# Weight sums of the Strassen products: adding DMAs from GpSimd's queue instead of VectorE

## The chip, the cores and the metric

The kernel runs on one core of a Trainium2 chip. The metric is the device time of one execution in microseconds (us), the median of several runs. The engines are called PE (TensorE, matmuls; PEld is its weight load), DVE (VectorE), ACT (ScalarE), POOL (GpSimd) and SP (SyncE, which here only issues DMAs). PEq, ACTq, SPq and POOLq are the instruction queues of these engines.

## The reference

A trunk of two layers over 512 tokens of width 1024, in float32. Each layer is a half-step feed-forward block, a mixer, a second half-step feed-forward block and a gated input embedding; a final norm follows.

```python
def swiglu(x, w_gu, w_down):
    g, u = jnp.split(x @ w_gu, 2, axis=-1)
    return (jax.nn.silu(g) * u) @ w_down
...
    for i in range(DEPTH):
        h = h + 0.5 * swiglu(rmsnorm(h, ffn1_norm[i]), ffn1_w_gu[i], ffn1_w_down[i])
        u = rmsnorm(h, mix_norm[i])
        b_g, c_g, v_c, q_c, kv_c, k_r, g_conv, g_mla = jnp.split(u @ w_in[i], split_pts, axis=-1)
        y_conv = short_conv_branch(b_g, c_g, v_c, conv_w[i], w_conv_out[i])
        y_mla = mla_branch(q_c, kv_c, k_r, ...)
        merged = jax.nn.sigmoid(g_conv) * y_conv + jax.nn.sigmoid(g_mla) * y_mla
        h = h + merged @ w_o[i]
        h = h + 0.5 * swiglu(rmsnorm(h, ffn2_norm[i]), ffn2_w_gu[i], ffn2_w_down[i])
        gate = jax.nn.sigmoid(rmsnorm(h, ple_norm[i]) @ w_ple_gate[i])
        h = h + gate * (p[i] @ w_ple_proj[i])
    return rmsnorm(h, final_norm)
```

What matters here are the products `x @ w_gu` of the four feed-forward blocks (w_gu is 1024 x 5632) and the two gate products of the mixer (columns g_conv and g_mla of w_in).

## The kernel before, in words

Activations are kept transposed: a tile holds 128 features (partitions) by 512 tokens. Every float32 operand is split into a high part (a cast to float32r, on ACT) and a low part (the difference, on DVE), and each product is made of three matmuls: high by high, high by low, low by high.

Weights lie in HBM as pieces of 128 x 1024 float32 (512 KB), in the order of their use. `Stream.raw` (L45) loads a piece from SP's queue into one of ten buffers, named `st` (`N_RAW`, L29); `Stream.split` (L61) casts it to `wh` on ACT (L67) and takes the difference `wl` on DVE (L68). There are four buffers each of `wh` and `wl` (`N_WH`), so the splits run at most some three pieces ahead of TensorE. A load waits until the split of the piece that held its buffer has read it.

Most of the gate and up products are made by the Strassen scheme in Winograd's form, seven products in place of eight. A unit of it, called a quad here, is four pieces of weights: the quarters a11, a21, a22, a12 of a block of 512 columns by 1024 rows (a first index for the group of columns, a second for the half of the rows). There are 47 quads: 9 in the first feed-forward block (named a0 in the profile), 10 in each of the other three (b0, a1, b1), 4 in each of the two mixers (m0, m1). The names of the products in PSUM have the block, the number of the quad and the letter of the bank: a07c is bank c of quad 7 in block a0.

The inputs of the seven products come from `Halved.row` (L353): sums and differences of the left and right 256 tokens of the upper and lower features, named x, y, t and u. `Quad.part(j)` (L119) gives the weights of product j and takes the weight sums on DVE: L127 makes `s` = a21 + a22 in a fifth buffer for product 5, L132 takes a11 from it for product 6, L135 takes `s` from a12 for product 3, L138 takes a21 from a11 for product 7. `Sevens.product` (L394) makes the 24 matmuls of 128 x 256 (L400), and `Sevens.step` (L403) gathers the results: products 1, 5 and 6 are copied out of PSUM on ACT (L419), products 2, 3 and 7 are added on DVE (L424), and four finished quarters of the output go to `finish` (L462) or `gate` (L611). There DVE multiplies by the row factor r of the norm (L466, L613), and ACT takes SiLU or sigmoid.

In a feed-forward block the products of neighbouring quads are woven into one another, with parts of the down projection between them (`down`, L479, 12 matmuls of 128 x 512 each):

```python
for i, (n_, j_) in enumerate(((n + 1, 1), (n, 7), (n + 1, 5), (n, 4), (n + 1, 2), (n + 1, 6), (n + 1, 3))):
    step(n_, j_)
    if i in (1, 2, 3, 5) and between:
        between.pop(0)()
```

So in the steady state, product 6 of a quad is followed by one `down`, then by product 3. The first quad of a block runs its products 1, 2, 5, 6, 3 in a row, and in b0, a1 and b1 the second quad has no `down` between its products, as `between` is still empty (n of 1, L515); there the inputs of the quads and the norm are also made. The mixer does the same with `conv_out` in place of `down`.

The order of each engine's instructions is fixed when the program is built, by a scheduler that follows the order of the text as a priority and lets an instruction pass that it expects to be ready sooner. At run time each engine goes through its own list in order.

Of the kernel before, what the change touches and what calls it, by code (L numbers as in the profile page):

```python
# [13 lines left out]
ALU = mybir.AluOpType  # L14
AX = mybir.AxisListType

P = 128
# [15 lines left out]
class Stream:  # L33


    def __init__(self, nc, src, sp, wp):
        self.nc, self.src, self.sp, self.wp = nc, src, sp, wp
        self.halves = []
        self.tiles = None
        self.ahead = []  # L40
# [70 lines left out]
class Quad:  # L111


    def __init__(self, W, quarters):
        self.W = W
        for q in ("a11", "a21", "a22", "a12"):
            setattr(self, q, W.raw(quarters[q]))

    def part(self, j):  # L119

        W = self.W
        tt = W.nc.vector.tensor_tensor
        if j == 1:
            return W.split(self.a11)
        if j == 5:
            self.s = W.buffer("s")
            tt(self.s, self.a21, self.a22, ALU.add)  # L127
            return W.split(self.s)
        if j == 2:
            return W.split(self.a12)  # L130
        if j == 6:
            tt(self.s, self.s, self.a11, ALU.subtract)  # L132
            return W.split(self.s)
        if j == 3:
            tt(self.a12, self.a12, self.s, ALU.subtract)  # L135
            return W.split(self.a12)
        if j == 7:
            tt(self.a11, self.a11, self.a21, ALU.subtract)  # L138
            return W.split(self.a11)
        return W.split(self.a22)  # L140


def pack(halves, n_halves, arrays):
# [15 lines left out]
def trunk_kernel(ctx, tc, dims, x, p, positions, gains, rope_c, weights, out):  # L159

    nc = tc.nc
    S, D, DEPTH, PD, DFF, CONV, QL, KL = dims
# [11 lines left out]
    W = Stream(nc, weights, sp, wp)  # L174

    def G(name, dt=F32):
        return gp.tile([P, S], dt, tag="g", name=name)
# [60 lines left out]
    def gain(nm, l, k):  # L238
        c = col_at[nm, l] + k
        return cols[:, c:c + 1]  # L240
# [4 lines left out]
    class Squares:  # L245
# [5 lines left out]
        def add(self, t):  # L251
            w = t.shape[1]
            if self.acc is None:
                self.acc = G(self.name + "acc")[:, :w]
                nc.scalar.activation(self.acc, t, AF.Square)
                return
            sq = G(self.name + "sq")[:, :w]
            nc.scalar.activation(sq, t, AF.Square)
            nc.vector.tensor_tensor(self.acc, self.acc, sq, ALU.add)
# [86 lines left out]
    class Halved:  # L346
# [6 lines left out]
        def row(self, j, xs):  # L353
            H = S // 2
            left, right = slice(0, H), slice(H, S)
            name, k = self.name, j + KD // 2

            def halves_of(hi_lo, *ps_):
                for at, p_ in zip((left, right), ps_):
                    if p_:  # L360
                        self.ys[p_].append(tuple(t[:, at] for t in hi_lo))

            xj, xk, t13, t24 = (G(f"{name}{w}{j}") for w in "xytu")
            nc.scalar.mul(xj, h[j], gain(self.nm, self.l, j))
            nc.scalar.mul(xk, h[k], gain(self.nm, self.l, k))
            halves_of(xs[j], 1, None)
            halves_of(xs[k], 2, 3)
            nc.vector.tensor_tensor(t13[:, left], xj[:, right], xj[:, left], ALU.subtract)
            nc.vector.tensor_tensor(t13[:, right], xk[:, right], xj[:, right], ALU.subtract)
            nc.vector.tensor_tensor(t24[:, left], t13[:, right], xj[:, left], ALU.add)  # L370
            nc.vector.tensor_tensor(t24[:, right], xk[:, left], t24[:, left], ALU.subtract)
            halves_of(split(t13, f"{name}t{j}"), 5, 7)
            halves_of(split(t24, f"{name}u{j}"), 6, 4)

    class Sevens:
# [5 lines left out]
        H = S // 2  # L381
# [21 lines left out]
        def step(self, n, j):  # L403
# [18 lines left out]
            else:  # L422
                i, f, c = {2: (1, 0, 0), 3: (6, 0, 1), 7: (5, 1, 1)}[j]
                nc.vector.tensor_tensor(d[i], ps, d[i], ALU.add)  # L424
                self.done(n, f, c, d[i], d[i])

    def ffn(l, nm, name, first=False, beside=None, early=False):
        H = S // 2
        nf = DFF // P
        W.close()  # L430
        acts = {}
        ys = Halved(nm, l, name)
        n_early = KD // 2 - 2 if early else 0

        def early_rows(k, xs):
            if KD // 2 < k + 1 <= KD // 2 + n_early:
                ys.row(k - KD // 2, xs)

        xs, acc = normed(nm, l, name, early_rows)


        n_whole = 4 if first else 2
        cs = [[W.col(nm + "_w_gu", l, c + f * P, D) for c in (0, DFF)] for f in range(n_whole)]
        names = [[f"{name}p{w}{f}" for w in "gu"] for f in range(n_whole)]
        n = 2 if first else 1
        pss = projs(sum(cs[:n], []), xs, sum(names[:n], []))
        r = rms(acc, D, name)
        for f in range(n, n_whole):
            pss += projs(cs[f], xs, names[f])
        for j in range(n_early, KD // 2):  # L450
            ys.row(j, xs)

        def activate(f):
            g, u = G(f"{name}gn{f}"), G(f"{name}un{f}")
            nc.vector.tensor_tensor(g, pss[2 * f], r, ALU.mult)
            nc.scalar.activation(g, g, AF.Silu)
            nc.vector.tensor_tensor(u, pss[2 * f + 1], r, ALU.mult)
            nc.vector.tensor_tensor(u, u, g, ALU.mult)
            acts[f] = split(u, f"{name}a{f}")


        def finish(n, f, c, src, t):  # L462

            i = 2 * n + f
            at = slice(c * H, (c + 1) * H)
            nc.vector.tensor_tensor(t, src, r[:, at].unsqueeze(1).to_broadcast([P, 2, H]), ALU.mult)  # L466
            nc.scalar.activation(t[:, 0, :], t[:, 0, :], AF.Silu)
            whole = i in acts
            if not whole:
                acts[i] = G(f"{name}an{i}")  # L470
            nc.vector.tensor_tensor(acts[i][:, at], t[:, 1, :], t[:, 0, :], ALU.mult)
            if whole:
                acts[i] = split(acts[i], f"{name}a{i}")

        sevens = Sevens(nm + "_w_gu", l, name, ys.ys, lambda n: [[c + (2 * n + a_) * P for c in (0, DFF)] for a_ in range(2)],
                        finish)
        step = sevens.step

        def down(m, f0, f1, ps=None, last=True, first_=True):  # L479
            ps = PS(f"{name}pd{f0}_{m}") if ps is None else ps  # L480
            for f in range(f0, f1):
                mm3(ps, W.get((nm + "_w_down", l, f * P, m * P)), acts[f], first_ and f == f0, last and f == f1 - 1)
            if last:
                nc.vector.scalar_tensor_tensor(h[m], ps, 0.5, h[m], ALU.mult, ALU.add)  # L484
            return ps

        np_ = nf // 2
        n0 = n_whole // 2
        for f in range(n_whole - 2):
            activate(f)  # L490
        step(n0, 1)
        activate(n_whole - 2)
        step(n0, 2)
        step(n0, 5)
        activate(n_whole - 1)
        step(n0, 6)
        step(n0, 3)
        for n in range(n0, np_):
            f0 = (n - 2) // 2 * 4
            if n == np_ - 1:  # L500

                pds = []
                for i, j in enumerate((7, 4, None)):
                    pds.append(down(i, f0, f0 + 4, last=False))
                    if j:
                        step(n, j)
                if beside:
                    beside()
                for m in range(KD):
                    if m < 3:  # L510
                        down(m, f0 + 4, nf, pds[m], first_=False)
                    else:
                        down(m, f0, nf)
                break
            between = [(lambda m=m, f0=f0: down(m, f0, f0 + 4)) for m in range(4 * (n % 2), 4 * (n % 2) + 4)] if n > 1 else []  # L515
# [4 lines that stand above are left out]
# [12 lines left out]
    def mixer(l):  # L532
# [32 lines left out]
        for k, (vh, vl) in enumerate(xs):  # L565
            if k % 4 == 0:
                wa, wb = W.halves_of(*kr_cols[k:k + 4])
            t = slice(k % 4 * P, (k % 4 + 1) * P)
            nc.tensor.matmul(pkr, wa[:, t], vh, start=k == 0, stop=False)
            nc.tensor.matmul(pkr, wb[:, t], vl, start=False, stop=k == KD - 1)  # L570
        r = rms(acc, D, name)
# [38 lines left out]

        def gate(n, f, c, src, t):  # L611
            at = slice(c * (S // 2), (c + 1) * (S // 2))
            nc.vector.tensor_tensor(t, src, r[:, at].unsqueeze(1).to_broadcast([P, 2, S // 2]), ALU.mult)  # L613
            for w in range(2):
                i = 4 * n + 2 * f + w
                if gates[i] is None:
                    gates[i] = G(f"{name}g{i}")
                nc.scalar.activation(gates[i][:, at], t[:, w, :], AF.Sigmoid)
# [149 lines left out]
        for m in range(KD):  # L768
            mla_part(m, N_HEADS - 2 if m < 3 else 0, N_HEADS)
            t = m_b[m]  # L770
# [172 lines left out]
```

## Time and profile before

| | us |
|---|---|
| median of 3 runs | 2305.26 (2304.94 to 2305.39) |
| the profiled execution's own time | 2305.14 |
| its span, first to last instruction | 2303.4 |
| TensorE busy | 2281.0 |
| VectorE busy | 1881.2 |
| ScalarE busy | 1129.3 |
| GpSimd busy | 36.8 |

The profile shows one execution. A row of the groups has the line, the engine, the operation, output and inputs, shape and count, then the busy time in us and the mean ns of one, then the idle time of the engine before it and what ended that. A row of the waits has the waiting engine, tile and line, what it waited for, the sum in us, the times, and the longest. A row of the timeline has the start and the duration in us. A row of the DMA issues has the size and the median us from issue to landing. The granted TensorE clock was 0.996 of full speed on average.

### The profile page before, as it was taken

Reading aid. Unit: us, or ns where it says so; the run is one execution under the profiler, and the core shown is the slowest. Engines: PE = TensorE matmul, PEld = TensorE weight load, DVE = VectorE, ACT = ScalarE, POOL = GpSimd, SP = SyncE. Lnnn points to the kernel's source line nnn. Section 1 sums busy time; section 2 is a strip of 40 time slices with the busy share of each in tenths; the row PEclk is TensorE's granted clock in tenths of the full one; section 3 lists DMA queues with packets and bytes.
Section 4 is the critical chain, followed back from the end, with each engine's and each line's share of the span. In section 5 each row is a group of like instructions: output and inputs, shape, how many; then the busy total and the mean of one; then the engine's idle time right before and its main releaser. Section 6 shows DMA issues by size and latency. Waiting matters only on the chain.

```text
span 2303.4 us, 34969 instructions
## 1 busy us (share of the span) xinstructions
PE 2281.0 (99%) x14272; PEld 2068.1 (90%) x14272; DVE 1881.2 (82%) x2613; ACT 1129.3 (49%) x1683; POOL 36.8 (2%) x42
## 2 busy tenths in 40 slices
PE   9999999999999999999999999999999999999997
PEld 7999988899888999998899999889988889999987
DVE  8978779978966988877898887689789579888776
ACT  7444444455644644444564444445466355444455
POOL 0000000000100000000000000000002000000000
PEclk9999999999999999999999999999999999999998
DMA  5333343233122233334223333322331213333341
GB/s 193 110 110 100 102 124 101 66 109 119 46 74 83 81 112 92 110 109 130 73 83 110 96 106 111 119 92 64 120 101 47 83 55 120 101 101 110 120 137 38
DMA packets 64529, 228.03 MB, mean 99 GB/s; under 512 B 7408, under 2 KB 7408, under 8 KB 64368
## 3 DMA queue, kind: packets, MB, share of 16 engines
q1 hardware_dynamic: 63936, 225.47, 31.5%
q8 instruction: 112, 1.84, 0.3%
q14 instruction: 49, 0.40, 0.1%
q10 hardware_dynamic: 432, 0.32, 0.0%
HBM read 223.66 MB, written 2.10 MB: 98 GB/s over the span
## 4 chain that ended last, share of the span: by engine, by line
PE 93%; DVE 5%; ACT 1%; issue 1%; DMA 0%; ACTq 0%; SPq 0%
PE a0pd L198 2%; PE b0pd L198 2%; PE b1pd L198 2%; PE a1pd L198 2%; PE a1pd L199 2%; PE b0pd L199 2%; PE a0pd L199 2%; PE b1pd L199 2%; PE a1pd L200 2%; PE b1pd L200 2%; PE a0pd L200 2%; PE b0pd L200 2%; DVE wl L68 1%; PE e1gp L198 1%; PE e1gp L199 1%; PE e1gp L200 1%
## 5 line engine op out<-in xcount | busy, mean ns | idle before, releaser
L67 ACT CAST wh<-st 128x1024 fp32r<-128x1024 f32 (+1 forms) x471 | 490.8, 1043 | 588.0 <-issue 66.4
L68 DVE TENSOR_TENSOR wl<-st,wh 128x1024 fp32r<-128x1024 f32 (+1 forms) x471 | 570.1, 1211 | 159.7 <-ACT wh L67 159.1
L67 ACT CAST wh<-s 128x1024 fp32r<-128x1024 f32 x94 | 98.8, 1051 | 120.2 <-PE b0pd L199 8.5
L68 DVE TENSOR_TENSOR wl<-s,wh 128x1024 fp32r<-128x1024 f32 x94 | 114.4, 1217 | 13.4 <-ACT wh L67 13.3
L135 DVE TENSOR_TENSOR st<-st,s 128x1024 f32<-128x1024 f32 x47 | 57.4, 1222 | 1.1
L132 DVE TENSOR_TENSOR s<-s,st 128x1024 f32<-128x1024 f32 x47 | 57.3, 1218 | 0.2
L138 DVE TENSOR_TENSOR st<-st,st 128x1024 f32<-128x1024 f32 x47 | 57.2, 1217 | 0.1
L127 DVE TENSOR_TENSOR s<-st,st 128x1024 f32<-128x1024 f32 x47 | 57.1, 1216 | 0.1
L484 DVE SCALAR_TENSOR_TENSOR h<-b0pd,h 128x512 f32<-128x512 f32 x40 | 27.5, 688 | 9.1 <-PE b0pd L200 9.1
L484 DVE SCALAR_TENSOR_TENSOR h<-b1pd,h 128x512 f32<-128x512 f32 x40 | 27.5, 688 | 9.1 <-PE b1pd L200 9.1
L484 DVE SCALAR_TENSOR_TENSOR h<-a1pd,h 128x512 f32<-128x512 f32 x40 | 27.5, 687 | 7.5 <-PE a1pd L200 7.5
L484 DVE SCALAR_TENSOR_TENSOR h<-a0pd,h 128x512 f32<-128x512 f32 x40 | 27.5, 687 | 6.4 <-PE a0pd L200 6.4
L103 POOL MEMSET wh<- 128x256 f32 x4 | 1.1, 314 | 1195.1 <-DVE wl L68 1195.1
L771 DVE TENSOR_TENSOR m0g<-m0mop,m0g 128x512 f32<-128x512 f32 x8 | 5.5, 691 | 6.5 <-PE m0mop L200 6.5
L771 DVE TENSOR_TENSOR m1g<-m1mop,m1g 128x512 f32<-128x512 f32 x8 | 5.5, 691 | 6.2 <-PE m1mop L200 6.2
L272 ACT ACT_TABLE_LOAD x8 | 10.3, 1283 | 0.1
L776 DVE TENSOR_TENSOR h<-m1wop,h 128x512 f32<-128x512 f32 x8 | 5.5, 691 | 4.1 <-PE m1wop L200 4.1
L776 DVE TENSOR_TENSOR h<-m0wop,h 128x512 f32<-128x512 f32 x8 | 5.5, 690 | 4.1 <-PE m0wop L200 4.1
L824 ACT ACTIVATE e_0g<-e_0g 128x512 f32<-128x512 f32 (+1 forms) x13 | 6.8, 529 | 2.8 <-DVE e_0g L823 2.7
L861 PE MATMUL ft<-ident,fh 128*128 128x128 f32 x32 | 5.9, 322 | 1.8 <-DVE fh L853 1.8
L198 PE MATMUL a0pg<-a0x0h,wh 128*128 128x512 f32 x4 | 2.2, 551 | 5.5 <-ACT a0x0h L193 5.5
L622 DVE TENSOR_TENSOR m0g<-m0cop,m0g 128x512 f32<-128x512 f32 x8 | 5.5, 690 | 2.5 <-PE m0cop L200 2.5
(11091 smaller groups left out, 8854.5 us busy)
## 6 DMA issues: line engine op xcount, KB each, us to landing
st<-in_weights SPq DMA_DIRECT2D x416, 512.0 KB, 3.6
st<-in_weights SPq DMA_DIRECT2D x8, 256.0 KB, 5.4
h<-in_x SPq DMA_DIRECT2D x8, 256.0 KB, 5.4
out<-fo SPq DMA_DIRECT2D x8, 256.0 KB, 2.3
e0pi<-in_p SPq DMA_DIRECT2D x2, 256.0 KB, 4.0
e1pi<-in_p SPq DMA_DIRECT2D x2, 256.0 KB, 3.8
pos_i<-in_positions ACTq DMA_DIRECT2D x1, 256.0 KB, 4.3
cols<-in_gains ACTq DMA_DIRECT2D x1, 53.0 KB, 2.9
```

What stands on the lines that cost most here:

```text
L67: self.nc.scalar.copy(hi[:, w], src[:, w])
L68: self.nc.vector.tensor_tensor(lo[:, w], src[:, w], hi[:, w].bitcast(F32), ALU.subtract)
L127: tt(self.s, self.a21, self.a22, ALU.add)
L132: tt(self.s, self.s, self.a11, ALU.subtract)
L135: tt(self.a12, self.a12, self.s, ALU.subtract)
L138: tt(self.a11, self.a11, self.a21, ALU.subtract)
L198: nc.tensor.matmul(ps, wh, vh, start=first, stop=False)
L199: nc.tensor.matmul(ps, wh, vl, start=False, stop=False)
L200: nc.tensor.matmul(ps, wl, vh, start=False, stop=last)
L484: nc.vector.scalar_tensor_tensor(h[m], ps, 0.5, h[m], ALU.mult, ALU.add)
L771: nc.vector.tensor_tensor(t, mla_ps[m], t, ALU.mult)
L776: nc.vector.tensor_tensor(h[m], ps, h[m], ALU.add)
```

## The change

The weight sums leave VectorE. `Quad.__init__` loads the four quarters as before, and then `s` is no buffer of its own but a21, into which a DMA from GpSimd's queue adds a22, read from HBM a second time (`accum_op`). After the split for product 1, a DMA adds a21 from HBM into a11, for product 7. After the split for product 5, one adds a11 into `s`, for product 6; after that for product 6, one adds a12 into `s`, for product 3. Each adds 512 KB. A DMA adds and does not subtract, so the signs move: the weights of products 5, 6, 3 and 7 are now sums alone, the input differences t and u are taken with the signs that belong to it, and the second half of each quad's outputs (f = 1) comes out with its sign reversed. `scaled` turns it back where the outputs are multiplied by the row factor. The instructions there and in `row` stay as many as before. The numbers of buffers and the order of the steps in the text are as before.

```diff
     def __init__(self, W, quarters):
-        self.W = W
+        self.W, self.at = W, {}
         for q in ("a11", "a21", "a22", "a12"):
+            self.at[q] = len(W.halves)
             setattr(self, q, W.raw(quarters[q]))
+        self.s = self.a21
+        self.add(self.s, "a22")
+
+    def add(self, t, q):
+        self.W.nc.gpsimd.dma_start(out=t, in_=self.W.src[self.at[q]], accum_op=ALU.add)
 
     def part(self, j):
 
         W = self.W
-        tt = W.nc.vector.tensor_tensor
         if j == 1:
-            return W.split(self.a11)
-        if j == 5:
-            self.s = W.buffer("s")
-            tt(self.s, self.a21, self.a22, ALU.add)
-            return W.split(self.s)
-        if j == 2:
-            return W.split(self.a12)
-        if j == 6:
-            tt(self.s, self.s, self.a11, ALU.subtract)
-            return W.split(self.s)
-        if j == 3:
-            tt(self.a12, self.a12, self.s, ALU.subtract)
-            return W.split(self.a12)
-        if j == 7:
-            tt(self.a11, self.a11, self.a21, ALU.subtract)
-            return W.split(self.a11)
-        return W.split(self.a22)
+            res = W.split(self.a11)
+            self.add(self.a11, "a21")
+            return res
+        if j in (5, 6):
+            res = W.split(self.s)
+            self.add(self.s, "a11" if j == 5 else "a12")
+            return res
+        return W.split({2: self.a12, 3: self.s, 7: self.a11, 4: self.a22}[j])
...
-            nc.vector.tensor_tensor(t13[:, left], xj[:, right], xj[:, left], ALU.subtract)
+            nc.vector.tensor_tensor(t13[:, left], xj[:, left], xj[:, right], ALU.subtract)
             nc.vector.tensor_tensor(t13[:, right], xk[:, right], xj[:, right], ALU.subtract)
-            nc.vector.tensor_tensor(t24[:, left], t13[:, right], xj[:, left], ALU.add)
-            nc.vector.tensor_tensor(t24[:, right], xk[:, left], t24[:, left], ALU.subtract)
+            nc.vector.scalar_tensor_tensor(t24[:, left], t13[:, right], -1.0, xj[:, left], ALU.mult, ALU.subtract)
+            nc.vector.scalar_tensor_tensor(t24[:, right], t24[:, left], -1.0, xk[:, left], ALU.mult, ALU.subtract)
...
+    def scaled(t, src, f, r):
+
+        r = r.unsqueeze(1).to_broadcast([P, 2, S // 2])
+        if f == 0:
+            nc.vector.tensor_tensor(t, src, r, ALU.mult)
+        else:
+            nc.vector.scalar_tensor_tensor(t, src, -1.0, r, ALU.mult, ALU.mult)
...
-            nc.vector.tensor_tensor(t, src, r[:, at].unsqueeze(1).to_broadcast([P, 2, H]), ALU.mult)
+            scaled(t, src, f, r[:, at])
...
-            nc.vector.tensor_tensor(t, src, r[:, at].unsqueeze(1).to_broadcast([P, 2, S // 2]), ALU.mult)
+            scaled(t, src, f, r[:, at])
```

## The prediction

> **What bounds the kernel now.** I read the head of the page first, then the waits of TensorE, then the groups of the lines that the change touches, then the timeline around one Strassen quad in the steady state and one at the start of a feed-forward block.
>
> ```profile
> span 2303.4 us, 34969 instructions
> PE 2281.0 (99%) x14272; PEld 2068.1 (90%) x14272; DVE 1881.2 (82%) x2613; ACT 1129.3 (49%) x1683; POOL 36.8 (2%) x42
> PE a0pg L198 <- ACT a0x0h L193: 5.5, 1, 5.5
> PE fss L850 <- DVE f0acc L259: 2.4, 1, 2.4
> PE fss L850 <- DVE f256acc L259: 1.9, 1, 1.9
> PE ft L861 <- DVE fh L853: 1.8, 2, 1.6
> ...
> PE b01c L400 <- ACT b01c L419: 0.6, 1, 0.6
> PE b11c L400 <- ACT b11c L419: 0.6, 1, 0.6
> PE a11b L400 <- DVE wl L68: 0.5, 1, 0.5
> ```
>
> TensorE is busy in 2281.0 of 2303.4 us. Its large waits are one at the start (5.5) and a few in the final norm (2.4, 1.9, 1.8). In the Strassen products (L400) it waits 0.6 + 0.6 + 0.5 = 1.7 us in all, each time at the start of a feed-forward block. VectorE is the second engine with 82%, but it is not what the end waits for. So the change takes work off an engine that hardly holds TensorE up, and it can give back little more than those 1.7 us, with small stalls beside them perhaps 3 us. The question is what the new DMAs cost.
>
> **What is removed.** The four weight sums of a quad, on VectorE:
>
> ```profile
> L135 DVE TENSOR_TENSOR st<-st,s 128x1024 f32<-128x1024 f32 x47 | 57.4, 1222 | 1.1
> L132 DVE TENSOR_TENSOR s<-s,st 128x1024 f32<-128x1024 f32 x47 | 57.3, 1218 | 0.2
> L138 DVE TENSOR_TENSOR st<-st,st 128x1024 f32<-128x1024 f32 x47 | 57.2, 1217 | 0.1
> L127 DVE TENSOR_TENSOR s<-st,st 128x1024 f32<-128x1024 f32 x47 | 57.1, 1216 | 0.1
> ```
>
> 57.4 + 57.3 + 57.2 + 57.1 = 229.0 us of VectorE work goes, 188 instructions in 47 quads. In the steady state none of it lies on the path that sets the end. At the start of a block it nearly does, as VectorE is full there:
>
> ```profile
> 762.00:800.00 38.00, 37.35 (x302) 36.52 (x301) 37.53 (x51) 24.14 (x35) 0.00 (x0) 1.00 0.29 87
> 830.00:1040.00 210.00, 210.00 (x1460) 196.75 (x1459) 167.95 (x203) 91.56 (x122) 0.00 (x0) 1.00 0.35 106
> ```
>
> The columns are the stretch, its length, then busy time of TensorE, its weight load, VectorE, ScalarE and GpSimd. In 762 to 800 us VectorE is busy 37.53 of 38.00 us and TensorE loses 0.65; in 830 to 1040 us VectorE has 42 us spare and TensorE loses nothing. The instructions that change their form (the reversed signs in `row` and `scaled`) keep their count and their elements, so I cost them at nothing.
>
> **What is added.** 188 DMAs of 512 KB on GpSimd's queue, each adding a quarter of the weights from HBM into a buffer in SBUF. The trace has no adding DMA, and none from GpSimd. The nearest rows are the plain loads of the same quarters from SyncE's queue:
>
> ```profile
> st<-in_weights SPq DMA_DIRECT2D x416, 512.0 KB, 3.6
> DMA to landing us min/median/max: 2.8/3.6/10.2
> q1 hardware_dynamic: 63936, 225.47, 31.5%
> ```
>
> A plain load lands 3.6 us after its issue, between 2.8 and 10.2 (the latter in the burst at the start). An adding DMA must also read its destination. The third row gives the packets of that queue, their MB and their share of 16 engines' time: a packet takes 31.5% x 16 x 2303.4 / 63936 = 0.18 us of one DMA engine, and a 512 KB load has 128 rows, 8 packets on each of 16 engines: 1.45 us. If the second read costs as much as the first, my estimate for an add, L, is 3.6 + 1.45 = 5.1 us; the ends are 2.8 (it costs no more than the quickest load) and 10.2 + 1.45 = 11.7. I take 5.1, since nearly all loads lie near their median. The share of the DMA engines rises by 188 x 2.9 us / 2303 = 24 points, from a third to a half or more: room enough.
>
> The Trainium skill ("DMA: Bandwidth & Descriptors", section on the anatomy of a DMA of the GpSimd path) fits such a DMA as 2.0 us plus its bytes at 436 GB/s. That would be 3.2 us for 512 KB, below the 3.6 us of the row, and an estimate of 4.4 us with the bytes counted twice; no trace here shows it, and by it each late product below would be 0.7 us less late.
>
> Three of the four adds have time: the one of a22 into a21 runs when both quarters are due long before product 5; that of a21 into a11 starts after product 1 is split and is used most of a period later by product 7; that of a11 lies between products 5 and 6, with other products between. If that cover were gone, each would cost what the next one may cost. The tight one is the add of a12 into `s`, between the split for product 6, which must have read `s`, and the split for product 3, which reads the sum. Before, L135 needed only the old `s`, so it ran ahead of the split. Now there is a chain. In the steady state:
>
> ```profile
> 205.37 1.05 ACT L67 CAST wh<-s 128x1024 fp32r<-128x1024 f32 x1 [1.06 <-PE a0pd L199]
> 206.86 1.22 DVE L68 TENSOR_TENSOR wl<-s,wh 128x1024 fp32r<-128x1024 f32 x1
> 208.39 1.05 ACT L67 CAST wh<-st 128x1024 fp32r<-128x1024 f32 x1 [1.97 <-PE a06b L400]
> 209.48 1.23 DVE L68 TENSOR_TENSOR wl<-st,wh 128x1024 fp32r<-128x1024 f32 x1 [0.31 <-ACT wh L67]
> ...
> 219.52 0.28 PE L400 MATMUL a07c<-a0x4h,wh 128*128 128x256 f32 x1
> ```
>
> The first two rows are the split for product 6 of quad 7, the next two that for product 3, the last the first matmul of product 3; its third matmul, 0.24 us later, needs the low part. `s` has been read at 208.08; a split takes 209.48 + 1.23 - 208.39 = 2.3 us. So L may be 219.52 + 0.24 - 208.08 - 2.3 = 9.4 us, some 9.1 with the hand-over, before TensorE waits. At 5.1 us the add is hidden with 4 us to spare. What queues behind the waiting cast on ScalarE (the SiLU of product 4, the copy of product 6) is needed later than product 3. On VectorE the low part of the split waits with it, and that engine has the freed 1.22 us slots. On GpSimd's queue a waiting add holds the next add, and GpSimd has only 36.8 us of other work. SyncE's loads stay on their own queue, and a quad now holds four buffers instead of five, so they come no later.
>
> At the start of a block the second quad has no `down` between products 6 and 3, and splits run less far ahead:
>
> ```profile
> 783.91 1.21 DVE L68 TENSOR_TENSOR wl<-st,wh 128x1024 fp32r<-128x1024 f32 x1
> 787.71 1.22 DVE L132 TENSOR_TENSOR s<-s,st 128x1024 f32<-128x1024 f32 x1
> 791.51 1.21 DVE L68 TENSOR_TENSOR wl<-s,wh 128x1024 fp32r<-128x1024 f32 x1
> ...
> 793.40 0.28 PE L400 MATMUL b02b<-b0u0h,wh 128*128 128x256 f32 x1
> 796.28 0.28 PE L400 MATMUL b02c<-b0x4h,wh 128*128 128x256 f32 x1
> 799.16 0.28 PE L400 MATMUL b03b<-b0x0h,wh 128*128 128x256 f32 x1
> ...
> 1925.59 1.21 DVE L68 TENSOR_TENSOR wl<-s,wh 128x1024 fp32r<-128x1024 f32 x1
> 1930.35 0.28 PE L400 MATMUL b12c<-b1x4h,wh 128*128 128x256 f32 x1
> ...
> 1184.16 1.22 DVE L68 TENSOR_TENSOR wl<-s,wh 128x1024 fp32r<-128x1024 f32 x1
> 1197.98 0.28 PE L400 MATMUL a12c<-a1x4h,wh 128*128 128x256 f32 x1
> 1165.21 1.21 DVE L68 TENSOR_TENSOR wl<-s,wh 128x1024 fp32r<-128x1024 f32 x1
> 1177.00 0.28 PE L400 MATMUL a12b<-a1x0h,wh 128*128 128x256 f32 x1
> 1177.24 0.28 PE L400 MATMUL a11c<-a1x4h,wh 128*128 128x256 f32 x1
> ```
>
> In b0, `s` is free for the add of a12 at 791.51 + 1.21 = 792.7; with L = 5.1 and the split's 2.3 the low part is there at 800.1, and product 3 wants it at 796.28 + 0.24: 3.6 us late if the order of the work stays. In b1 the same from 1926.8: 3.6. In a1 two adds follow the split for product 5, done at 1185.4: 1185.4 + 2 x (5.1 + 2.3) = 1200.2, against 1198.2: 2.0. For the first quad of a1, 1166.4 + 14.8 = 1181.2 against 1177.5: 3.7. Sum with the order kept: 3.6 + 3.6 + 2.0 + 3.7 = 12.9 us. But the order of the work is no fixed text: the last two rows show a matmul of the next quad's product 1 (a12b) ahead of product 3 (a11c), so work that is ready is put into such gaps when the program is laid out. In b0 the next quad's product 1 stands at 799.16, right behind, 2.88 us long (799.16 - 796.28). Put ahead four times it covers 2.9 + 2.9 + 2.0 + 2.9 = 10.7 of the 12.9 us. About 2 us stay.
>
> **The sum**, against the profiled execution's own 2305.14 us (span 2303.4 and 1.7 around it; the median of the runs, 2305.26, is the same within 0.01%): nothing in the steady state, about 2 us more and 1.7 us less at the starts. I allow 1.5 us for uneven landings: 2307.
>
> **The rivals.** A measurement of this kernel can tell about 0.2% from no change, 4.6 us.
>
> First, slower, at the starts: the adds take longer than the layout of the program allowed for, so no product is moved ahead and every late split is paid. With 5.1 us that is 12.9 us, 2318; with L = 8 each add makes a product 2.9 us later, twice where two adds follow one another, some 6 times: 12.9 + 17 = 30, 2335. Against it stands the filling in the rows above; for it, that VectorE's fullness there makes splits late already. The Trainium skill's page "SBUF — State Buffer" (section on who interferes with whom) speaks against the change here: a VectorE instruction in a two-port mode keeps GpSimd from writing descriptors. No run here shows it yet. By the rows a wait for one VectorE instruction in progress is up to 1.22 us, which makes L 6.3: hidden in the steady state, and 5 to 7 us more in this case (1.22 us at the four late products, twice at two of them).
>
> Second, slower, in the steady state: if L passes 9.1 us, product 3 waits in every quad with a `down` before it, 36 of the 47 (8 or 9 in each of four blocks, one or two in each mixer). It decides from 9.1 on: at the upper end, 11.7, it is 2.6 x 36 = 94 us, 2399. If the add ran at a quarter of a load's rate or in many small pieces, L would be 15 or more and the price over 200 us. For it speaks that nothing in the trace shows an adding DMA; against it that even the slowest load took 10.2.
>
> Third, faster: VectorE is no longer full at the starts, and the waits there (1.7 us, and the 0.65 us of each such stretch) go; with adds near the lower end, 2.8 us, nothing is late. That is 2305.1 - 3 = 2302, still within what can be told; over 4.6 us would need gains that TensorE's waits do not hold.
>
> **How the numbers follow.** Hidden, within 0.2%: 0.47. Late at the starts: 0.25, slower. Late in the steady state: 0.20, slower, and 0.03 of it far above. Faster by over 0.2%: 0.05; the remaining 0.03, for a cost that I have not named (the start and end of GpSimd's queue), goes to slower. So faster 0.05, same 0.47, slower 0.48: the likeliest single case is no change, 2307, with its own range of 2301 to 2309.7; slower has as much chance spread over two cases. The range that holds 8 in 10 runs from 2301 to 2400: below it lie few of the faster cases, above it the longest adds, 0.12 or so.
>
> **What would show it.** VectorE's busy time falls by 229 us to about 1652, TensorE's stays at 2281. Adds land in about 5 us. TensorE shows no wait before product 3 in the steady state, and waits of a few us at most at 760 to 800, 1160 to 1204 and 1896 to 1934 us. Wrong would be landings over 9 us with a wait before product 3 in each period; a product order at the starts that is unchanged; or ScalarE's casts waiting for DMAs long enough that later splits are late too.

## The result and the profile after

The change makes the kernel slower: 2345.62 us (median of 4 runs, 2343.57 to 2347.05) against 2305.32 us, a ratio of 1.0175 with a 95% interval of 1.0162 to 1.0188. The profiled execution's span is 2345.1 us against 2303.4, 41.7 us more. Two executions on record took far longer than all the others (3793.81 us of the run with useless matmuls below, 7995.75 us of the kernel before); the ratios leave them out.

From the page of the changed kernel: the span, the busy time, the new DMA queue (packets, MB, share of 16 engines) and the issues; the last row, from the view of line L123, has the landing of the adds.

```profile
span 2345.1 us, 35365 instructions
PE 2296.3 (98%) x14272; PEld 2082.1 (89%) x14272; DVE 1683.1 (72%) x2425; ACT 1124.0 (48%) x1683; POOL 200.6 (9%) x230
q0 software_dynamic: 27072, 98.58, 24.4%
st<-in_weights SPq DMA_DIRECT2D x416, 512.0 KB, 4.0
st<-in_weights POOLq DMA_DIRECT2D x188, 512.0 KB, 5.7
DMA to landing us min/median/max: 5.2/5.7/10.8
```

VectorE lost 198 us of work, TensorE got 15 us more busy with the same 14272 matmuls, and an add lands 5.7 us after its issue. TensorE's waits (engine, tile, line, what it waited for: us, times, longest) say where the time went:

```profile
PE a11c L396 <- ACT wh L67: 4.3, 1, 4.3
PE b01c L396 <- ACT wh L67: 4.2, 1, 4.2
PE b11c L396 <- ACT wh L67: 3.9, 1, 3.9
PE m1g0c L396 <- ACT m1g0c L415: 3.8, 1, 3.8
PE m0g0c L396 <- ACT m0g0c L415: 3.8, 1, 3.8
PE a02c L396 <- ACT a02c L415: 3.6, 1, 3.6
...
PE a12c L396 <- ACT wh L67: 2.3, 1, 2.3
```

These are single waits, one in each of the six blocks, all ahead of product 3 of the block's first quad, and one more in the second quad of a1. Short waits for the low part of the same split follow (0.5 to 0.7 us in four of these places), and b02c and b12c wait 0.2 us for theirs; the view lists none in the other quads. Busy time by stretch (length, TensorE, its weight load, VectorE, ScalarE, GpSimd, then the granted clock, the DMA share and GB/s):

```profile
466.00:482.00 16.00, 12.21 (x89) 12.00 (x88) 9.21 (x10) 10.16 (x14) 1.73 (x2) 0.89 0.70 156
785.00:800.00 15.00, 10.09 (x61) 9.62 (x60) 10.11 (x13) 7.71 (x10) 1.73 (x2) 0.77 0.63 138
1221.00:1232.00 11.00, 8.15 (x43) 7.79 (x43) 8.58 (x12) 6.79 (x10) 1.76 (x2) 0.69 0.59 119
200.00:330.00 130.00, 130.00 (x891) 121.17 (x890) 86.37 (x110) 55.85 (x75) 10.46 (x12) 1.00 0.63 163
```

In the steady state (200 to 330 us) TensorE is busy throughout, with the DMA engines at 63% where they were at 36%. At the starts it waits, and after the wait it runs at a lower granted clock: a mean of 0.77 over 15 us is 6.8 us at half speed. So it is in the second quad of a1 (1221 to 1232 us), where the wait is only 2.3 us. Taking for each matmul the time to the next one's start above the usual one of its shape, the trace has 47.8 us in gaps of over 0.15 us (17.2 before) and 17.7 us in smaller ones (6.6 before): 30.5 us of waits and 11.0 us of slow matmuls make up the 41.7. The mean granted clock fell from 0.996 to 0.988, which is 19 us of lost clock; a part of it lies in the waits themselves, where it costs nothing.

The chain at the start of b0, from the timelines of VectorE, GpSimd, ScalarE and TensorE:

```profile
772.56 1.22 DVE L68 TENSOR_TENSOR wl<-st,wh 128x1024 fp32r<-128x1024 f32 x1
774.42 0.88 POOL L123 DMA_DIRECT2D st<-in_weights  x1 [13.99 <-DVE b0u2l L187]
780.22 1.05 ACT L67 CAST wh<-st 128x1024 fp32r<-128x1024 f32 x1 [3.10 <-DMA st<-in_weights]
781.30 1.23 DVE L68 TENSOR_TENSOR wl<-st,wh 128x1024 fp32r<-128x1024 f32 x1 [2.75 <-ACT wh L67]
782.93 0.87 POOL L123 DMA_DIRECT2D st<-in_weights  x1 [7.63 <-DVE wl L68]
788.59 1.04 ACT L67 CAST wh<-st 128x1024 fp32r<-128x1024 f32 x1 [3.13 <-DMA st<-in_weights]
789.69 0.39 PE L396 MATMUL b01c<-b0x4h,wh 128*128 128x256 f32 x1 [4.21 <-ACT wh L67]
790.95 0.58 PE L396 MATMUL b01c<-b0x4h,wl 128*128 128x256 f32 x1 [0.70 <-DVE wl L68]
```

The split for product 5 ends at 773.8; the add of a11 (774.42) has landed when ScalarE casts at 780.22; that split ends at 782.5; the add of a12 goes out at 782.93 and the cast for product 3 runs at 788.59. Two adds of 5.7 us and two splits stand in a row, and TensorE, which finished product 6 at 785.5, waits for the end of it. Its next matmuls, which before the change filled such a place (the next quad's product 1 ran ahead of product 3 in b0), now stand behind product 3, and the casts that they would need stand behind the waiting cast on ScalarE.

### The profile page after: what moved, and what is told of

The parts are those of the page before. It is cut to its first block, busy times and chain, and to the rows that moved or that the text cites. A ratio compares the mean times of both kernels' runs of the same rounds, so it can differ in the third digit from the quotient of the medians.

```text
span 2345.1 us, 35365 instructions
## 1 busy us (share of the span) xinstructions
PE 2296.3 (98%) x14272; PEld 2082.1 (89%) x14272; DVE 1683.1 (72%) x2425; ACT 1124.0 (48%) x1683; POOL 200.6 (9%) x230
## 5 line engine op out<-in xcount | busy, mean ns | idle before, releaser
L68 DVE TENSOR_TENSOR wl<-st,wh 128x1024 fp32r<-128x1024 f32 (+1 forms) x565 | 685.3, 1214 | 383.4 <-ACT wh L67 382.3
L67 ACT CAST wh<-st 128x1024 fp32r<-128x1024 f32 (+1 forms) x565 | 584.6, 1043 | 709.2 <-DMA st<-in_weights 176.3
L123 POOL DMA_DIRECT2D st<-in_weights x188 | 163.8, 872 | 1698.9 <-DVE wl L68 733.7
L626 DVE TENSOR_TENSOR m1g<-m1cop,m1g 128x512 f32<-128x512 f32 x8 | 5.5, 690 | 4.3 <-PE m1cop L196 4.3
L830 DVE TENSOR_TENSOR h<-h,e_0g 128x512 f32<-128x512 f32 (+1 forms) x13 | 7.2, 561 | 0.0
```

Source lines behind the costliest of these rows:

```text
L67: self.nc.scalar.copy(hi[:, w], src[:, w])
L68: self.nc.vector.tensor_tensor(lo[:, w], src[:, w], hi[:, w].bitcast(F32), ALU.subtract)
L123: self.W.nc.gpsimd.dma_start(out=t, in_=self.W.src[self.at[q]], accum_op=ALU.add)
L626: nc.vector.tensor_tensor(gates[m], ps, gates[m], ALU.mult)
```

## The experiments

The theory: the loss is the latency of a chain of two adds at the start of each block, with the lower clock behind each wait. The rivals: each adding DMA costs something wherever it stands (traffic, GpSimd, the loads it delays); the new signs or another layout of the program cost the time; or, for the size of it, the adding itself costs nothing and GpSimd's queue all.

**The change without its DMAs.** All four sums as `tensor_tensor` with `ALU.add` on VectorE, with the new signs:

```diff
+        if self.dve and j in (5, 6, 3, 7):
...
+            tt(t, a, b, ALU.add)
+            return W.split(t)
...
-            return {"w": Quad(W, quarters)}
+            return {"w": Quad(W, quarters, len(self.todo) < 99)}
```

> All weight sums on VectorE, with the new signs, the reversed second half of the outputs and no DMA from GpSimd: the change without its DMAs. Theory: signs cost nothing, 2304 to 2307 us. Rival (the sign forms of the instructions on VectorE, or another layout of the program, cost part of the 41.7 us): above 2310 us.

Measured: 2305.09 us, ratio 1.0001 (0.9991 to 1.0010). The signs and `scaled` cost nothing; the DMAs make the whole loss.

**The first quad, and the first two, of each block on VectorE.** The same edit, with another limit:

```diff
-            return {"w": Quad(W, quarters)}
+            return {"w": Quad(W, quarters, len(self.todo) < 1)}
```

> The first quad of each of the six blocks takes its weight sums on VectorE again (sums only, with the new signs and a fifth buffer), the other 41 quads keep their adding DMAs. Theory (the chain of two adds at the start of a block): the waits ahead of product 3 of the first quads go, 4 to 8 us in each of six blocks with the slowed matmuls behind them, and only what lies in the second quads is left, about 5 us in a1 and up to 4 each in b0 and b1: 2306 to 2318 us. Rival (each adding DMA costs something, by contention or on GpSimd): 41 of 47 quads keep theirs, so 41/47 of the 41.7 us stay: about 2342 us.

Measured: 2327.01 us, ratio 1.0099 (1.0082 to 1.0116): between the two, slower than the theory's range. The waits ahead of product 3 are gone from the first quads and stand in the second ones, each with 0.8 us more for the low part and 3.4 us at half clock behind it. In the changed kernel the delay of the first quad had given the second ones time:

```profile
PE b12c L408 <- ACT wh L67: 3.9, 1, 3.9
PE a12c L408 <- ACT wh L67: 3.3, 1, 3.3
PE b02c L408 <- ACT wh L67: 2.7, 1, 2.7
```

With two quads (`len(self.todo) < 2`), which leaves 35 adding quads:

> The first two quads of each block take their sums on VectorE, the other 35 keep the adding DMAs. Theory: nothing is late any more, 2304 to 2308 us, with VectorE busy some 60 us longer than in the changed kernel. Rival of a cost in each adding DMA: 35/47 of 41.7 us stay, about 2336 us.

Measured: 2305.30 us, ratio 1.0003 (0.9993 to 1.0012). 140 adding DMAs, all behind the first two quads of a block, cost nothing that can be measured. That ends the rival of a cost in each DMA.

**One link of the chain on VectorE.** First the second link, the add of a12, in a12's own buffer as before the change:

```diff
+        if j == 3:
+            W.nc.vector.tensor_tensor(self.a12, self.a12, self.s, ALU.add)
...
```

> Of the four adds only that of a12 goes back to VectorE, into the buffer of a12, so that it does not wait for the split of product 6; the other three stay DMAs in all quads. Theory: the second link of the chain is gone; product 3 is late no more, product 6 by 0.3 to 1 us in some blocks: 2305 to 2314 us. Rival of a cost in each adding DMA: 3/4 of 41.7 us stay, about 2336 us.

Measured: 2320.48 us, ratio 1.0068 (1.0053 to 1.0083), less than the rival's figure, but 6 us over the theory's range. The first link alone still makes product 3 wait, by way of an engine's order: in b0 and b1 TensorE waits 1.9 us each for ScalarE's copy of product 5 out of PSUM, a02c 1.6. The rest lies in waits of 1.1 to 1.2 us, for the split of product 6 in the first quad of a1 and in the second of b0, and for ScalarE's cast of an input of product 5 in m0 and m1, with two stretches of 3.4 us at half clock. Then the first link, the add of a11:

```diff
+        if j == 6:
+            W.nc.vector.tensor_tensor(self.s, self.s, self.a11, ALU.add)
...
```

> Of the four adds that of a11 into s, between products 5 and 6, goes back to VectorE; the other three stay DMAs (that of a21 into a11 after it). Theory of the chain of two links: one link stays, so the waits ahead of product 3 fall by the part that the first link added; a single link of 5.7 us between products 6 and 3 leaves some 3 to 4 us in most starts: 2318 to 2332 us. Rival (the second link alone makes the whole loss): 2345 us.

Measured: 2328.23 us, ratio 1.0099 (1.0083 to 1.0115), in the theory's range, but the waits are not where it had them. Ahead of product 3 of the first quads they are 0.6 to 1.9 us. In b0, a1 and b1 the layout of this run starts the next quad's product 1 ahead of product 3, and it is that product 1 which waits, 3.3, 2.3 and 2.7 us. In b0:

```profile
PE b02b L398 <- ACT wh L67: 3.3, 1, 3.3
780.87 1.04 ACT L67 CAST wh<-st 128x1024 fp32r<-128x1024 f32 x1 [4.20 <-DMA st<-in_weights]
782.66 1.98 ACT L67 CAST wh<-st 128x1024 fp32r<-128x1024 f32 x2
783.74 0.58 PE L398 MATMUL b02b<-b0x0h,wh 128*128 128x256 f32 x1 [3.34 <-ACT wh L67]
```

ScalarE's cast for product 3 waits for the add until 780.87, and the cast for product 1 stands behind it: the work that was to fill the gap is held by the same wait. Left alone, the first link makes about 15 us of loss and the second about 23; both together make 40.

**A plain copy in place of the add.** This leaves the sums out: the DMAs overwrite.

```diff
-        self.W.nc.gpsimd.dma_start(out=t, in_=self.W.src[self.at[q]], accum_op=ALU.add)
+        self.W.nc.gpsimd.dma_start(out=t, in_=self.W.src[self.at[q]])
```

> The same 188 DMAs from GpSimd's queue as plain copies: they overwrite and do not add, so the sums are left out. Theory: landing falls from 5.7 us by the second read, 1.45 us by the packet count, to about 4.3; two links at the start of each block are each 1.4 us shorter, so waits there fall by 2 to 3 us in six blocks, and some slowed matmuls with them: 2320 to 2332 us. Rival (the adding costs nothing and the queue all): landing stays at 5.7 and the time at 2345 us.

Measured: 2312.13 us, ratio 1.0034 (1.0021 to 1.0047). From the issues and the view of L123 in this run:

```profile
st<-in_weights POOLq DMA_DIRECT2D x188, 512.0 KB, 3.9
L123 POOL DMA_DIRECT2D st<-in_weights x188: 527/527/677, 23.0 to 2172.7; - x188
```

Adding costs 5.7 - 3.9 = 1.8 us of landing, of which 0.34 us are GpSimd's own time on the instruction (865 ns in the changed kernel, 527 here). Those 1.8 us in each link are worth 33 us of the kernel's time, more than the theory gave them: by the sums used above, the waits fall from 30.5 to about 5 us, some 4 us in each block, and the 11 us of slow matmuls go with them. One stretch of 3.4 us at half clock is left, behind the waits of 1.8 and 0.8 us in a1.

**The add of a12 twice.** The sum then has a12 in it twice.

```diff
             self.add(self.s, "a11" if j == 5 else "a12")
+            if j == 6:
+                self.add(self.s, "a12")
```

> The add of a12 is made twice, one after the other (a12 counts twice in the sum), so that the link between products 6 and 3 is some 11.5 us long in all quads. Theory (the steady state bears 9.1 us): product 3 waits about 2.4 us in 36 quads, 86 us, and the starts are 6 us later in six blocks with slowed matmuls, 36 to 60 us: 2460 to 2500 us. Rival (the steady state bears more, because the splits run further ahead or another product fills the gap): only the starts pay, 2380 to 2410 us.

Measured: 2531.83 us, ratio 1.0985 (1.0968 to 1.1001). In the steady state, from the timelines of VectorE, GpSimd, ScalarE and TensorE:

```profile
228.84 1.23 DVE L68 TENSOR_TENSOR wl<-st,wh 128x1024 fp32r<-128x1024 f32 x1 [0.17 <-ACT wh L67]
230.47 0.86 POOL L123 DMA_DIRECT2D st<-in_weights  x1 [12.79 <-DVE wl L68]
236.38 0.88 POOL L123 DMA_DIRECT2D st<-in_weights  x1 [5.05 <-DMA st<-in_weights]
241.97 1.04 ACT L67 CAST wh<-st 128x1024 fp32r<-128x1024 f32 x1 [8.86 <-DMA st<-in_weights]
243.07 0.39 PE L398 MATMUL a07c<-a0x4h,wh 128*128 128x256 f32 x1 [1.01 <-ACT wh L67]
```

From the read of `s` (230.07) to the cast (241.97) the link is 11.9 us, and product 3, which TensorE would have begun at 241.9, waits for its high part to 243.07 and then 0.8 us for the low part. The waits ahead of product 3, taken from the gaps as above, come to 81 us in 33 quads of the steady state, 2.5 each, as the theory had it (2.4 in 36). The time is above its range all the same, for two reasons. At the starts the waits alone grow by some 62 us over the changed kernel, where the theory had 36 to 60 with the slow matmuls: first quads wait 6 to 10 us, and second ones 4.8 to 6.6 us in five blocks. And the clock falls in the steady state too, behind some of these waits of 2 to 3 us:

```profile
200.00:330.00 130.00, 122.91 (x823) 113.36 (x822) 78.20 (x99) 51.68 (x70) 15.68 (x18) 0.97 0.70 167
```

Of the 49 us of slow matmuls that this run has over the kernel before, 31 lie there, where the theory had none.

**Useless matmuls in the wait.** 32 matmuls of 128x256, which nothing reads, ahead of product 3 of each first quad:

```diff
+            if j == 3 and n == min(self.todo):
+                warm = PS(nn + "warm")
+                for i in range(32):
+                    nc.tensor.matmul(warm[:, :self.H], ones, self.ys[1][i % 4][0], start=True, stop=True)
```

> The changed kernel with 32 matmuls of 128x256 that nothing reads, 3.8 us of work, ahead of product 3 of the first quad of each block. Theory (the wait of some 4 us is followed by a lower granted clock, which makes about 11 to 15 us of the 41.7): the matmuls fill the waits, the clock stays at full speed in five blocks, and the kernel gets faster by added work: 2330 to 2338 us. Rival (the slow matmuls come from something else, such as late operands): no gain, 2345 us, or up to 23 us more where the fill is not covered by a wait.

Measured: 2345.4 us, ratio 1.0175 (1.0158 to 1.0192): no gain, as the rival had it, yet not for its reason. The stretches that had a lower clock have none now:

```profile
466.00:482.00 16.00, 16.00 (x134) 15.82 (x133) 10.01 (x11) 10.18 (x15) 1.74 (x2) 1.00 0.71 168
785.00:800.00 15.00, 13.95 (x114) 13.55 (x114) 11.68 (x14) 8.84 (x12) 1.73 (x2) 1.00 0.67 153
```

So the clock did follow the waits in these places. In sum the filling put in 6 x 3.8 = 23 us of work, took 19 us of waits and 5 us of slow matmuls out, and the second quads, now in time to be late, waited 1.4 to 1.9 us and had a lower clock in their turn. That 192 matmuls come at no cost shows the waits, but a net price for the clock can't be had from it.

**Product 5's copy on VectorE.**

```diff
-                nc.scalar.copy(d[j], ps)
+                if j == 5:
+                    nc.vector.tensor_copy(d[j], ps)
+                else:
+                    nc.scalar.copy(d[j], ps)
```

> The changed kernel with one move: product 5 is copied out of PSUM on VectorE, not on ScalarE. Theory (in a0, m0 and m1 product 3 waits for that copy, which stands on ScalarE behind a cast that waits for the add of a12): the waits on the copy, 3.6 + 3.8 + 3.8 us, fall to the cast's own, under 1.5 us each, while b0, a1 and b1, which wait for the cast, keep theirs: 2332 to 2340 us. Rival (the add itself is the last to arrive everywhere, the copy is only the one named): 2345 us.

Measured: 2346.48 us, ratio 1.0185 (1.0169 to 1.0202): the rival's time. In the waits, m0g0c now waits 3.3 us for the copy on VectorE where it waited 3.8 us for it on ScalarE:

```profile
PE m1g0c L396 <- DVE m1g0c L416: 3.7, 1, 3.7
PE a02c L396 <- DVE a02c L416: 3.6, 1, 3.6
PE m0g0c L396 <- DVE m0g0c L416: 3.3, 1, 3.3
```

The copy still comes last: on VectorE it stands behind two splits, which wait for the same casts. So the move did not take the copy out of the line behind the add, and whether a copy outside that line would help a0, m0 and m1 stays open.

**Time between the links.** All adds stay DMAs. Product 5 comes first, and product 3 of the first quad after the next quad's product 1 and its own product 7 (in the mixer alike):

```diff
-        step(n0, 1)
+        step(n0, 5)
         activate(n_whole - 2)
+        step(n0, 1)
         step(n0, 2)
-        step(n0, 5)
         activate(n_whole - 1)
         step(n0, 6)
-        step(n0, 3)
...
                 step(n_, j_)
+                if n == n0 and i == 1:
+                    step(n0, 3)
```

> All four adds stay DMAs; only the order of the steps at the start of a block changes: product 5 first, then 1, 2, 6, and product 3 of the first quad after the next quad's product 1 and its own product 7. Theory (time between the links is what lacks): 6 has two products more ahead of it and 3 has two products between, 5.8 us each, about one add, so the waits of the first quads shrink to 1 or 2 us each: 2306 to 2316 us, unless ScalarE's casts wait in order for the add. Rival of a cost in each adding DMA: 2345 us as before.

Measured: 2305.86 us, ratio 1.0005 (0.9995 to 1.0014): the whole loss is gone with not one DMA less, only a little better than the theory's range. Product 5 first and product 3 later were not tried apart. Then product 3 of the second quad too, after the third quad's product 1 (in the mixer alike):

```diff
+                if n == n0 and i == 6:
+                    continue
                 step(n_, j_)
...
+                if n == n0 + 1 and i == 0:
+                    step(n0 + 1, 3)
```

> The order of the run before (product 5 first, product 3 of the first quad later), and product 3 of the second quad also later, after the next quad's product 1. All adds stay DMAs. Theory: the second quads' waits of 2.9 us in all go too, and with them all waits of the Strassen products: 2303 to 2305 us, the time before or a touch under it, as TensorE's own work is the bound. Rival (each adding DMA costs a little everywhere): 2306 us and up.

Measured: 2302.12 us, ratio 0.9987 (0.9978 to 0.9996): faster than both kernels, by 2.9 us against before. All waits of TensorE in it:

```profile
PE a0pg L194 <- ACT a0x0h L189: 5.7, 1, 5.7
PE fss L865 <- DVE f0acc L255: 2.5, 1, 2.5
PE fss L865 <- DVE f256acc L255: 1.9, 1, 1.9
PE ft L876 <- DVE fh L868: 1.8, 2, 1.6
PE m0s10p L721 <- DVE m0h1qn1l L187: 0.9, 1, 0.9
PE m1s10p L721 <- DVE m1h1qn1l L187: 0.9, 1, 0.9
```

None in a Strassen product is left in the view. Last, the same order with all sums on VectorE:

> The order of steps of the run before this one (product 5 first, product 3 of the first two quads later), with all weight sums on VectorE and no DMA from GpSimd. It tells whether the 2.9 us gained there come from the order alone. If from the order: 2301.5 to 2303 us again. If the adding DMAs bring it, by taking 1.22 us instructions from a VectorE that is full at the starts: 2304 to 2306 us, with TensorE's short waits at the starts of b0, a1 and b1 still there.

Measured: 2316.32 us, ratio 1.0048 (1.0033 to 1.0062), slower than either case expected. TensorE waits for VectorE's splits at the starts of b0, b1 (2.0 us each) and a1 (1.9 us), where VectorE is nearly full. The first of these two rows shows it in b0; the second is from the run before, with the DMAs:

```profile
762.00:800.00 38.00, 35.42 (x268) 34.40 (x267) 36.13 (x52) 22.11 (x31) 0.00 (x0) 0.96 0.22 70
762.00:800.00 38.00, 37.93 (x306) 37.34 (x305) 31.38 (x44) 23.90 (x34) 4.37 (x5) 1.00 0.61 142
```

So the gain needs both: the order gives the adds their time, and the adds take VectorE from 36.13 to 31.38 us of these 38.

## Why the prediction was right and wrong

Right: the time lies in the range (2301 to 2400), slower had 0.48, and the case that came true was the first rival, late at the starts. Wrong: the forecast itself, no change at 2307 us. That the range held the time is in part luck. It went to 2400 for the sake of adds of 11.7 us in the steady state, which did not come; the first rival's own sum, with the add at its measured 5.7 us, is 12.9 + 6 x 0.6 = 16.5 us, 2322, against 41.7 measured. By its steps:

- **What goes.** 229 us of sums left VectorE. Its busy time fell by 198 us and not by 229, with 188 instructions less: the rows of before overlap one another by about 0.08 us where they follow without a gap (L138 in b0 runs from 797.06 for 1.21 us, and the next row starts at 798.19), so that a busy time which counts each moment once held less of them than their sum. All such overlaps on VectorE came to 137 us before and 110 us after. It gave nothing back by itself. Right, and the run with two quads on VectorE shows the same from the other side.
- **The price of an add.** Estimated 5.1, measured 5.7 us. The second read was put at 1.45 us; adding costs 1.8. A plain DMA from GpSimd lands in 3.9 us, near SyncE's 3.6 before. The Trainium skill's fit ("DMA: Bandwidth & Descriptors", anatomy of the GpSimd path) gives an estimate of 3.2 us for that, and of 4.4 with the bytes counted twice; both are low against the 3.9 and 5.7 of the runs.
- **The steady state.** Hidden with 4 us to spare was right. The threshold of 9.1 to 9.4 us holds: a link of 11.9 us made product 3 late by some 2.5 us in 33 quads. The second rival's mechanism is real and begins where it was put, but the add is too quick for it.
- **VectorE against GpSimd's descriptors.** GpSimd's part of an add is 853 to 1095 ns in all 188, with VectorE busy 72% of the time, so no wait of 1.22 us shows. The rule that the prediction takes from the Trainium skill ("SBUF — State Buffer", section on who interferes with whom) is for instructions in a two-port mode, and that section says that `tensor_tensor` has none; the sums and the splits on VectorE are `tensor_tensor`, so the rule gave no reason for this price.
- **The step that failed**: "Put ahead four times it covers 10.7 of the 12.9 us. About 2 us stay." The evidence for it was thin: of the next quad's product 1, whose matmul was seen ahead of product 3 in a1, only 2 of the 24 matmuls stood there (1177.00 and 1177.12 us). Work that is ready was then not put into the gaps. The layout put product 3 right behind product 6 in b0, where before it had put the next quad's product 1 between, and where a layout did put it ahead (the run with the add of a11 on VectorE), product 1 waited itself, 3.3 us in b0, as its cast stood on ScalarE behind the cast that waits for the add. With product 5 put first and product 3 later by hand the loss is gone, which shows that the filling was possible and did not come by itself.
- **Places left out.** I counted 3.6, 3.6 and 2.0 us for second quads and 3.7 for one first quad. Six first quads waited, 3.6 to 4.3 us each; a0, m0 and m1 are not in the sum at all, nor are the first quads of b0 and b1. For these the premise "with other products between" does not hold: a first quad runs products 5, 6 and 3 in a row, so both links count. The second quads of b0, b1 and a1 waited 2.7, 3.9 and 3.3 us, and 0.8 more for the low part, only in the run in which the first quads are not late. So the sum was right for b0 and too small for b1 and a1.
- **A term that was not there at all**: 11 us of slow matmuls. Behind most of the waits ahead of product 3 TensorE's granted clock falls to half for 3.4 or 6.8 us. The Trainium skill ("TensorE: Matmul & The Clock Gate", Part 1) has the clock fall to half after an idle window of about 3.4 us. Here shorter waits did it too, and the length of the wait does not decide it: in the changed kernel waits of 3.8 to 4.3 us in five blocks were followed by it and so was that of 2.3 us in a1, while that of 3.6 us in a0 was not. In the run with the new order and all sums on VectorE, of two waits of 2.0 us ahead of the same product, the one in b0 (first row, granted clock 0.86) was followed by it and the one in b1 (second row, 1.00) was not:

```profile
784.00:796.00 12.00, 10.04 (x71) 9.84 (x70) 10.75 (x15) 5.61 (x10) 0.00 (x0) 0.86 0.30 89
1926.00:1938.00 12.00, 10.04 (x83) 9.83 (x83) 12.00 (x17) 5.88 (x10) 0.00 (x0) 1.00 0.30 89
```

In the trace's record of the clock the slow stretches of the changed kernel's starts begin at 472.56, 790.00, 1196.18, 1223.49, 1629.67 and 1947.12 us, whole multiples of 3.41 us apart. That fits fixed intervals of 3.41 us of which a large enough part was idle, so that where a wait falls counts as well as its length; no run here tests this.

With the right list the first rival's sum is 23.6 us for six first quads, 4.9 for second quads and low parts, and 11.0 for the clock: 39.5 of the 41.7 us.

What stays open: which of the two moves, product 5 first or product 3 later, took the loss away; how much of the waits in a0, m0 and m1 comes from the copy of product 5 in line behind the cast, and why the layout with VectorE's sums does so badly with the new order, beyond that VectorE is full there.

## What to carry to other kernels

Work that moves from an engine to a DMA changes its latency more than its cost: find the place where two such steps follow one another with the least work between, which is the start of a block and not the steady state, and put other work between them by hand. An engine that is not the bound holds up others through its order: what stands behind a waiting instruction waits as well, and a scheduler's filling should not be counted on before it is seen in the trace. A wait of TensorE of 2 us or more should be priced with the slow matmuls that can follow it: in the changed kernel 11.0 us with 30.5 us of waits, about a third more.

## What the runs showed that was not expected

- An adding DMA of 512 KB from GpSimd's queue lands in 5.7 us (5.2 to 10.8), a plain one in 3.9 (3.6 to 8.2); GpSimd is held for 0.87 and 0.53 us.
- 98.6 MB more DMA traffic, from 31.5% to 53% of the 16 engines' time on the two queues, moved the median landing of SyncE's loads only from 3.6 to 4.0 us. In the last order of steps with all 188 adds it cost TensorE nothing (2302.12 us). With plain copies of the same bytes the two queues took 44% and SyncE's loads stayed at 3.6 us.
- 1.8 us less in each of the two links were worth 33 us.
- Waits of TensorE of about 2 us can be followed by 3.4 or 6.8 us at half clock, and a wait of 3.6 us by none.
